# Filter-tap products regrouped by depth, four weight-split subtractions on GpSimd, and two small moves around them

## The chip, the cores and the metric

One core of a Trainium2 chip runs the whole layer as one program. The metric is the device time of one execution in microseconds (us); the median of three runs is given. One further execution was taken with the hardware profiler, and every row below is from that one.

## The reference, cut to what matters

The layer is a diffusion backbone block over 1024 tokens of width 1024, with 256 context tokens: normalisation, two parallel token mixers (a long convolution called Hyena and a recurrent mLSTM), a merge, then routing of tokens to 16 experts and a last normalisation. Four places matter here.

```python
# (1) the long filters: a small MLP gives h, its last layer is a product with w3
h = (h @ f32(w3)).reshape(L, HYENA_ORDER, 2, D_HYENA)
return h * jnp.exp(-t * deltas)[:, None, None, :]
# (2) routing: each of 16 experts takes its 128 best tokens
gate, idx = lax.top_k(jnp.swapaxes(aff, 1, 2), cap)
xg = h[bidx, idx]
# (3) the experts
a = jnp.einsum('becd,edf->becf', xg, w1); b = jnp.einsum('becd,edf->becf', xg, w3)
ye = jnp.einsum('becf,efd->becd', jax.nn.silu(a) * b, w2) * gate[..., None]
# (4) the last normalisation
return rmsnorm(x, final_norm_g)       # x * rsqrt(mean(x*x) + 1e-6) * g
```

## The kernel before, in words

Every large product runs on TensorE (PE) in three passes: an operand is split into a rounded high part and the remainder as low part, and high times high, high times low and low times high are summed in PSUM. A split is a cast on ScalarE (ACT) and a subtraction on VectorE (DVE) or GpSimd (POOL). PSUM has eight tiles of 128x512, which all stages share (`ps()`, line 125).

**Filters.** Eight units (kind, order, half of the channels) are made one after the other. `filter_taps` (line 384) makes a unit's taps: four PSUM tiles with two pairs of products each. Every pair is one product over 128 partitions (`hl` with `whh`) followed by one over 64 partitions (`hl` with `wll`, partitions 0 to 63 for the first four, 64 to 127 for the last four) into the same half of the tile. Each full tile is scaled out of PSUM by DVE (`fsf`), rounded by ACT and subtracted (`fs`; on DVE for the first unit, on POOL for the others). `filter_dft` (line 417) turns the taps into four PSUM tiles `fe`, and `filter_out` (line 437) combines these on DVE and POOL into `fk`, which goes to memory. `unit(u)` (line 555) runs the transform of unit u, the taps of unit u+2 and the output of unit u, with other small jobs interleaved (`ada`, the projection of the condition vector; the norms and transposes of the tokens). From the second unit on, the order of each engine's instructions is the planner's: it draws them by readiness and program order (`in_order[0] = False`, line 549); PE's order is the planner's from the start (`pe_order`).

**Routing.** The top 128 of each expert are found by DVE alone, sixteen rounds of MAX8, MATCH_REPLACE8 and FIND_INDEX8 (line 625 on). POOL then gathers the first expert's tokens by an indirect DMA (`gather`, line 1751), PE transposes them, and `gather_T` (line 1757) gives for each half n four scaled copies by ACT (`xgf`), a cast (`xgh`) and a subtraction (`xgl`).

**Experts.** 384 weight slabs of 1 MB flow through a ring of 11 tiles (`er`); `fill` (line 1724) splits each into `eh` (ACT) and `el` (DVE; only slab 2 on POOL). The first four slabs are split while the routing runs, ahead of `gather(0)` in program order. From line 1845 on, all engines keep program order until the last expert.

**Last norm.** For eight token tiles `xf` the sums of squares are made on ACT; `rsqrt` (line 477) for each pair of tiles is a chain of scale, square root on ACT, reciprocal, two multiplications, scale and multiplication on DVE; `last` (line 1923) scales the tiles, of which tiles 0, 2 and 4 are multiplied by the norm's weights on POOL, and stores them by the queue of SP.

Of the kernel before, what the change touches and what calls it, by code (L numbers as in the profile page):

```python
# [10 lines left out]
F32 = mybir.dt.float32  # L11
# [4 lines left out]
AF = mybir.ActivationFunctionType  # L16
OP = mybir.AluOpType
# [4 lines left out]
D = 1024  # L22
# [6 lines left out]
EPS = 1e-6  # L29
# [74 lines left out]
def layer_kernel(ctx: ExitStack, tc: tile.TileContext, A: dict, out: bass.AP, dbg=None, stop=None):  # L104
    nc = tc.nc
    in_order, pe_order = [True], [False]
    V, S, G = (InOrder(tc, e, in_order) for e in (nc.vector, nc.scalar, nc.gpsimd))
    T = InOrder(tc, nc.tensor, pe_order)
# [8 lines left out]
    def phase(st, name, side=None):  # L117

        pool = st.enter_context(tc.tile_pool(name=name, bufs=1, reuse_waits="tile", side=side))

        def alloc(shape, dt=F32, name=None, tag=None, bufs=1):
            return pool.tile(shape, dt, name=name, tag=tag or name, bufs=bufs)
        return alloc

    def ps(name="ps"):
        return pp.tile([128, 512], F32, name=name, tag="ps")

    def w2(shape, dt=F32, name="w"):
        return wk.tile(shape, dt, name=name, tag="w2", bufs=12)

    def sm(shape, name="sm"):
        return wk.tile(shape, F32, name=name, tag="sm", bufs=16)
# [14 lines left out]
    def bcast_row(ap, n):  # L147

        return bass.AP(tensor=ap.tensor, offset=ap.offset, ap=[[0, 128], [1, n]])

    def flat(name):
        a = A[name]
        n = 1
        for s in a.shape:
            n *= s
        return bass.AP(tensor=a.tensor, offset=a.offset, ap=[[1, n]])
# [227 lines left out]
    def filter_taps(u, al):  # L384

        kind, o, hf = u
        sets = [[al([128, 4, 256], F32R, name="fs", tag=f"ss{units.index(u) % 2}", bufs=4) for _ in range(2)] for _ in range(2)]
        filt["taps", u] = sets
        hl, whh, wll = filt["hl"], filt["whh"], filt["wll"]
        cs = slice(hf * 256, (hf + 1) * 256)  # L390
        for j2 in range(4):
            p = ps()
            h_ = slice(64 * (j2 // 2), 64 * (j2 // 2) + 64)
            for j in range(2):
                jt = j2 * 2 + j
                pj = p[:, j * 256:(j + 1) * 256]
                T.matmul(pj, hl[:, jt * 128:(jt + 1) * 128], whh[:, o, kind, cs], start=True, stop=False)
                T.matmul(pj, hl[h_, jt * 128:(jt + 1) * 128], wll[h_, o, kind, cs], start=False, stop=True)
            f = w2([128, 2, 256], name="fsf")
            js = slice((j2 % 2) * 2, (j2 % 2) * 2 + 2)  # L400
            V.scalar_tensor_tensor(f, p.rearrange("p (j c) -> p j c", j=2), -1.0 if kind and j2 > 1 else 1.0,
                                   filt["dec"][:, j2 * 2:j2 * 2 + 2, cs], op0=OP.mult, op1=OP.mult)
            if kind == 0 and j2 == 0:
                V.tensor_tensor(f[0:1, 0, :], f[0:1, 0, :], filt["skip"][:, o, cs], op=OP.add)
            hi, lo = sets[j2 // 2]
            S.copy(hi[:, js], f)
            (V if u == units[0] else G).tensor_tensor(lo[:, js], f, hi[:, js].bitcast(F32), op=OP.subtract)
            yield
# [68 lines left out]
    def rsqrt(ss, n, inv):  # L477

        v = sm([128, n], name="rq_v")
        V.tensor_scalar(v, ss, inv, EPS, op0=OP.mult, op1=OP.add)  # L480
        r = sm([128, n], name="rq_r")
        S.activation(r, v, AF.Sqrt)
        V.reciprocal(r, r)
        V.tensor_tensor(v, v, r, op=OP.mult)
        V.tensor_tensor(v, v, r, op=OP.mult)
        V.tensor_scalar(v, v, -0.5, 1.5, op0=OP.mult, op1=OP.add)
        V.tensor_tensor(r, r, v, op=OP.mult)
        return r
# [20 lines left out]
    late = phase(ctx, "late")  # L509
# [28 lines left out]
    def norm_tokens(*ii):  # L538
# [7 lines left out]
        yield  # L546

    run((filter_taps(units[0], alB), 1))
    in_order[0] = False
    filt["last_layer"](1)  # L550
# [491 lines left out]
    f = flat("b_in")  # L1042
# [90 lines left out]
    AB2 = late([128, 2, 8], F32, name="AB2")  # L1133
# [10 lines left out]
    p = ps()  # L1144
# [335 lines left out]
    for i in range(16):  # L1480
        p = ps()
# [17 lines left out]
    xs = []  # L1499
# [74 lines left out]
    for q in range(2):  # L1574
        for tt in range(8):
# [3 lines left out]
            i = q * 8 + tt  # L1579
# [38 lines left out]
    p = ps()  # L1618
# [27 lines left out]
    p = ps()  # L1646
# [17 lines left out]
    RAW, PAIR = 11, 4  # L1664
# [7 lines left out]
    def raw_tile(i):  # L1672
        return slot("er", i, RAW, [128, 2, 1024])

    def pair_tiles(i):
        return slot("eh", i, PAIR, [128, 2, 1024], F32R), slot("el", i, PAIR, [128, 2, 1024], F32R)
# [25 lines left out]
    def one(name, shape, dt=F32):  # L1702
        t = ring.pop((name,), None)
        return al(shape, dt, name=name) if t is None else t
# [16 lines left out]
    raws, pairs = [], []  # L1721
    taken = [0]

    def fill(n):

        while True:
            while len(raws) < min(len(pairs) + RAW, len(slabs)):
                raw = raw_tile(len(raws))
                SY.dma_start(raw, slabs[len(raws)].rearrange("(k p) n -> p k n", p=128))
                raws.append(raw)  # L1730
            i = len(pairs)
            if i >= min(n + PAIR, len(slabs)):
                return
            hi, lo = pair_tiles(i)
            S.copy(hi, raws[i])
            (G if i == 2 else V).tensor_tensor(lo, raws[i], hi.bitcast(F32), op=OP.subtract)
            pairs.append((hi, lo))


# [11 lines left out]
    def gather(e):  # L1751
        xg = one("xg", [128, 1024])
        G.indirect_dma_start(out=xg, out_offset=None, in_=xn_d,
                             in_offset=bass.IndirectOffsetOnAxis(ap=idxc[:, e:e + 1], axis=0))
        return xg

    def gather_T(xg):

        gh, gl = one("xgh", [128, 8, 128], F32R), one("xgl", [128, 8, 128], F32R)
        for n in range(2):  # L1760
            p = ps()
            for k in range(4):
                T.transpose(p[:, k * 128:(k + 1) * 128], xg[:, (n * 4 + k) * 128:(n * 4 + k + 1) * 128], ident)
            f = w2([128, 4, 128], name="xgf")
            ks = slice(n * 4, n * 4 + 4)

            def high(p=p, f=f, n=n, ks=ks):
                for k in range(4):
                    kk = n * 4 + k
                    S.activation(f[:, k], p[:, k * 128:(k + 1) * 128], AF.Identity, scale=AB2[:, 0, kk:kk + 1],  # L1770
                                 bias=AB2[:, 1, kk:kk + 1])
                S.copy(gh[:, ks], f)

            on_act.append(high)
            on_dve.append(lambda f=f, ks=ks: V.tensor_tensor(gl[:, ks], f, gh[:, ks].bitcast(F32), op=OP.subtract))
        return gh, gl
# [58 lines left out]

    fill(0)
    xg = gather(0)
    xs = {0: gather_T(xg)}
    for todo in (on_act, on_dve):
        while todo:  # L1840
            todo.pop(0)()
# [4 lines left out]
    for i in range(len(steps) + 1):  # L1846
        if i < len(steps):
            e, h = steps[i]
            if h == 0 and e + 1 < NE:
                xg = gather(e + 1)  # L1850
# [32 lines left out]
    def spare(shape, dt=F32, name=None):  # L1883

        n_raw[0] += 1
        return al(shape, dt, name=name, tag=f"er{(n_raw[0] - 1) % RAW}")

    warm = late([128, 1], F32, name="warm")
    tg = spare([128, 2, 1024], name="tg")
    SY.dma_start(tg[:, 0], bcast_row(A["tok"], 1024))  # L1890
    xf = []
    for i in range(4):
        t = spare([128, 2, 1024], name="xf")
        for j in range(2):
            tt = 2 * i + j
# [12 lines left out]
    sq = spare([128, 8, 2], name="sq")  # L1908

    later, rs2 = [], {}  # L1910
# [6 lines left out]
    def parts(tt):  # L1917

        if tt not in held:
            return [(xf[tt], slice(0, 1024))]  # L1920
        return [(held[tt][n], slice(n * 512, (n + 1) * 512)) for n in range(2)]
# [19 lines left out]
    for tt in range(8):  # L1941
        xt, on_pe = xf[tt], tt in (0, 7)
        if on_pe:
            held[tt] = [ps(), ps()]
            for n in range(2):
                T.matmul(held[tt][n], ident, xt[:, n * 512:(n + 1) * 512], start=True, stop=False)
        for n in range(2):
            p = held[tt][n] if on_pe else ps()
            for v in range(2):
                T.matmul(p, hot[:, tt * 128:(tt + 1) * 128], yhl[:, v, n], start=(v == 0 and not on_pe), stop=(v == 1))  # L1950
            if not on_pe:
                V.tensor_tensor(xt[:, n * 512:(n + 1) * 512], p, xt[:, n * 512:(n + 1) * 512], op=OP.add)
        for i, (src, ns) in enumerate(parts(tt)):
            S.activation(w2([128, 1024], BF16, name="junk")[:, ns], src, AF.Square, accum_out=sq[:, tt, i:i + 1])
        if on_pe:
            V.tensor_tensor(sq[:, tt, 0:1], sq[:, tt, 0:1], sq[:, tt, 1:2], op=OP.add)
        if tt % 2 == 1:
            rs2[tt - 1] = rsqrt(sq[:, tt - 1:tt + 1, 0], 2, 1.0 / D)
            if tt > 1:
                last(tt - 3)  # L1960
    last(6)
# [25 lines left out]
```

## Time and profile before

| what | value |
|---|---|
| median of three runs | 2297.56 us (2296.01 to 2298.42) |
| the profiled execution, its own time | 2295.03 us |
| its span, first to last instruction | 2293.3 us |
| PE busy | 2172.0 us, 95% |
| DVE busy | 1687.1 us, 74% |
| ACT busy | 1246.8 us, 54% |
| POOL busy | 443.5 us, 19% |

The profiled execution is 2.5 us below the median, and 1.7 us of it lie outside the span. A busy PE can be a PE that waits inside its pipeline, since ends of matmuls are modelled; so its share says little, and the steps between the starts of neighbouring products say more. In a row of a timeline stand the start in us, the duration, the engine, the operation with the tiles it writes and reads, the shape, the count, and in brackets the idle time of that engine before it with what ended it. In a table of stretches stand the stretch, its length, the busy time of PE, of PE's weight loads (PEld), DVE, ACT and POOL, each with its count, then PE's granted clock, the DMA share and GB/s; an engine with nothing in any stretch has no column.

### The profile page before, as it was taken

To read this page: it belongs to the slowest core of one execution; us is meant where nothing else is said; L and a number is where in the kernel's file an instruction comes from. 1 tells how busy PE (TensorE), PEld (TensorE's weight loads), DVE (VectorE), ACT (ScalarE), POOL (GpSimd) and SP (SyncE) were. 2 spreads that over 40 slices of the span, in tenths; PEclk is the share of its full clock that TensorE was granted. 3 is DMA by queue.
4 is the path that set the end of the run, shared out by engine and by line. 5 is a ranking of instruction groups with operands and counts; after the bars stand their busy time and mean duration, and the time that the engine had idled before them with its cause. 6 is when DMAs were issued, how large, how long until landed. Compare 5 with 4: busy or idle time off the path is not lost. (4 is left out here: it accounts for less than half of the span.)

```text
span 2293.3 us, 28327 instructions
## 1 busy us (share of the span) xinstructions
PE 2172.0 (95%) x10609; PEld 1772.4 (77%) x10609; DVE 1687.1 (74%) x1863; ACT 1246.8 (54%) x1398; POOL 443.5 (19%) x382
## 2 busy tenths in 40 slices
PE   6999999999999999999379999999999999999996
PEld 3679887787778788887268888888888888888884
DVE  5784445664446768553869889898888898888897
ACT  2441342324542223222257777777877777777774
POOL 3563101111124544042200111100111100011001
PEclk9879999999999999999689999999999999999998
DMA  7243335555563333864769999999999999999993
GB/s 264 93 139 95 113 114 176 176 195 190 177 199 114 110 115 124 300 223 147 271 216 386 380 386 382 378 379 393 381 385 384 379 377 396 380 386 383 380 349 141
DMA packets 234793, 605.18 MB, mean 264 GB/s; under 512 B 17722, under 2 KB 89462, under 8 KB 231456
## 3 DMA queue, kind: packets, MB, share of 16 engines
q1 hardware_dynamic: 216752, 551.44, 65.7%
q0 software_dynamic: 12128, 41.43, 5.7%
q10 hardware_dynamic: 5776, 10.50, 1.2%
q8 instruction: 83, 1.36, 0.2%
q14 instruction: 54, 0.44, 0.1%
HBM read 539.34 MB, written 63.98 MB: 263 GB/s over the span
## 5 line engine op out<-in xcount | busy, mean ns | idle before, releaser
L98 DVE TENSOR_TENSOR el<-er,eh 128x2048 fp32r<-128x2048 f32 x383 | 874.4, 2290 | 115.4 <-ACT eh L98 102.5
L98 ACT CAST eh<-er 128x2048 fp32r<-128x2048 f32 x384 | 733.7, 1915 | 236.6 <-PE pup L98 169.1
L98 PE MATMUL pup<-eh,xgh 128*128 128x512 f32 x1024 | 319.7, 393 | 1.6 <-ACT xgh L98 1.6
L98 PE MATMUL pup<-eh,xgl 128*128 128x512 f32 x1024 | 316.7, 390 | 0.0
L98 PE MATMUL ps<-hx,whi 128*128 128x512 f32 x960 | 305.4, 399 | 0.0
L98 PE MATMUL pup<-el,xgh 128*128 128x512 f32 x1024 | 274.4, 390 | 0.0
L98 PEld LDWEIGHTS pup<-eh,xgl 128*128 128x128 f32 x1024 | 192.7, 188 | 40.9 <-DVE xgl L98 0.2
L98 PEld LDWEIGHTS pup<-el,xgh 128*128 128x128 f32 x1024 | 192.6, 188 | 40.4
L98 PEld LDWEIGHTS pup<-eh,xgh 128*128 128x128 f32 x1024 | 190.3, 188 | 40.4 <-ACT xgh L98 2.0
L98 PEld LDWEIGHTS ps<-hx,whi 128*128 128x128 f32 x960 | 178.8, 189 | 40.3 <-ACT nt L98 0.8
L98 POOL DMA_INDIRECT acc_d<-ye,idxc x15 | 50.8, 3390 | 747.5 <-DVE ye L98 747.5
L98 PE MATMUL ps<-hx,wlo 128*128 128x512 f32 x480 | 189.9, 396 | 0.0
L98 PE MATMUL acc<-eh,gh 128*128 128x512 f32 x512 | 161.6, 397 | 0.2 <-ACT gh L98 0.2
L98 PE MATMUL acc<-eh,gl 128*128 128x512 f32 x512 | 160.2, 394 | 0.0
L98 PE MATMUL acc<-el,gh 128*128 128x512 f32 x512 | 139.5, 394 | 0.0
L98 PEld LDWEIGHTS acc<-eh,gl 128*128 128x128 f32 x512 | 96.0, 188 | 22.9 <-DVE gl L98 0.4
L98 PEld LDWEIGHTS acc<-el,gh 128*128 128x128 f32 x512 | 96.2, 188 | 22.4
L98 PEld LDWEIGHTS acc<-eh,gh 128*128 128x128 f32 x512 | 95.0, 188 | 21.6 <-ACT gh L98 0.5
L98 PEld LDWEIGHTS ps<-hx,wlo 128*128 128x128 f32 x480 | 90.5, 188 | 21.2
L98 PE MATMUL pg<-hx,gwh 128*128 128x512 f32 x320 | 103.2, 405 | 3.7 <-ACT gwh L98 3.7
L98 ACT ACTIVATE pb<-ps,colv 128x512 f32<-128x512 f32 (+1 forms) x44 | 29.3, 665 | 129.9 <-PE ps L98 122.2
L98 POOL DMA_INDIRECT xg<-xn_d,idxc x16 | 44.9, 2806 | 260.2 <-PE ps L98 226.1
(374 smaller groups left out, 3393.2 us busy)
## 6 DMA issues: line engine op xcount, KB each, us to landing
er<-in_w_exp_dram SPq DMA_DIRECT2D x384, 1024.0 KB, 7.6
wada<-in_w_ada_dram SPq DMA_DIRECT2D x24, 1024.0 KB, 5.0
wraw<-in_w_in_dram SPq DMA_DIRECT2D x30, 512.0 KB, 4.3
K_d<-fk SPq DMA_DIRECT2D x32, 256.0 KB, 2.2
Kt<-K_d SPq DMA_DIRECT2D x16, 512.0 KB, 5.7
v1c<-v_d SPq DMA_DIRECT2D x20, 256.0 KB, 8.0
gwr<-in_w_in_dram SPq DMA_DIRECT2D x20, 256.0 KB, 6.3
eo_d<-eost POOLq DMA_DIRECT2D x16, 256.0 KB, 7.0
```

What stands on the lines that cost most here:

```text
L98: r = op(*a, **k)
```

## The change

Four edits. In `filter_taps` all four PSUM tiles of a unit are taken at once, and its eight products over 128 partitions come first, then the eight over 64; only the first product of a tile sets the start flag. In `fill`, the subtractions of the first four slabs are all on POOL. In the first expert's `gather_T`, the four scaled copies of the second half are made by DVE instead of ACT. In the last norm a variant `rsqrt_s` takes the scale and the last affine step to ACT, each reading a constant tile `cs2`.

```diff
         hl, whh, wll = filt["hl"], filt["whh"], filt["wll"]
         cs = slice(hf * 256, (hf + 1) * 256)
+        pt = [ps() for _ in range(4)]
+
+        def tap(jt, high):
+            pj = pt[jt // 2][:, (jt % 2) * 256:(jt % 2 + 1) * 256]
+            h_ = slice(0, 128) if high else slice(64 * (jt // 4), 64 * (jt // 4) + 64)
+            T.matmul(pj, hl[h_, jt * 128:(jt + 1) * 128], (whh if high else wll)[h_, o, kind, cs], start=high and jt % 2 == 0, stop=not high and jt % 2 == 1)
+
+        for high in (True, False):
+            for jt in range(8):
+                tap(jt, high)
         for j2 in range(4):
-            p = ps()
-            h_ = slice(64 * (j2 // 2), 64 * (j2 // 2) + 64)
-            for j in range(2):
-                jt = j2 * 2 + j
-                pj = p[:, j * 256:(j + 1) * 256]
-                T.matmul(pj, hl[:, jt * 128:(jt + 1) * 128], whh[:, o, kind, cs], start=True, stop=False)
-                T.matmul(pj, hl[h_, jt * 128:(jt + 1) * 128], wll[h_, o, kind, cs], start=False, stop=True)
+            p = pt[j2]
...
             S.copy(hi, raws[i])
-            (G if i == 2 else V).tensor_tensor(lo, raws[i], hi.bitcast(F32), op=OP.subtract)
+            (G if i < PAIR else V).tensor_tensor(lo, raws[i], hi.bitcast(F32), op=OP.subtract)
...
-    def gather_T(xg):
+    def gather_T(xg, on=(True, True)):
...
-                    S.activation(f[:, k], p[:, k * 128:(k + 1) * 128], AF.Identity, scale=AB2[:, 0, kk:kk + 1],
-                                 bias=AB2[:, 1, kk:kk + 1])
+                    src, sc, sh = p[:, k * 128:(k + 1) * 128], AB2[:, 0, kk:kk + 1], AB2[:, 1, kk:kk + 1]
+                    if on[n]:
+                        S.activation(f[:, k], src, AF.Identity, scale=sc, bias=sh)
+                    else:
+                        V.tensor_scalar(f[:, k], src, sc, sh, op0=OP.mult, op1=OP.add)
...
-    xs = {0: gather_T(xg)}
+    xs = {0: gather_T(xg, (True, False))}
...
+    cs2 = late([128, 2], F32, name="cs2")
+    V.memset(cs2[:, 0:1], EPS)
+    V.memset(cs2[:, 1:2], 1.5)
+
+    def rsqrt_s(ss, n, inv):
+
+        v, r = sm([128, n], name="rq_v"), sm([128, n], name="rq_r")
+        S.activation(r, ss, AF.Sqrt, scale=inv, bias=cs2[:, 0:1])
+        S.activation(v, ss, AF.Identity, scale=inv, bias=cs2[:, 0:1])
+        V.reciprocal(r, r)
+        V.tensor_tensor(v, v, r, op=OP.mult)
+        V.tensor_tensor(v, v, r, op=OP.mult)
+        S.activation(v, v, AF.Identity, scale=-0.5, bias=cs2[:, 1:2])
+        V.tensor_tensor(r, r, v, op=OP.mult)
+        return r
...
-            rs2[tt - 1] = rsqrt(sq[:, tt - 1:tt + 1, 0], 2, 1.0 / D)
+            rs2[tt - 1] = rsqrt_s(sq[:, tt - 1:tt + 1, 0], 2, 1.0 / D)
```

## Rows read from the trace of the kernel before

**Rows 1.** A table of four stretches, all instructions (columns as told above).
```profile
54.00:90.00 36.00, 36.00 (x182) 23.26 (x180) 21.03 (x35) 13.90 (x25) 17.62 (x14) 0.91 0.43 150
90.00:121.00 31.00, 26.82 (x142) 21.42 (x142) 29.16 (x54) 14.13 (x29) 17.25 (x15) 0.76 0.21 69
121.00:146.00 25.00, 25.00 (x108) 19.77 (x108) 15.55 (x27) 12.77 (x23) 17.20 (x15) 0.70 0.25 85
146.00:184.00 38.00, 32.77 (x252) 31.54 (x251) 37.63 (x53) 20.52 (x29) 21.87 (x17) 0.94 0.61 182
```
**Rows 2.** PE's timeline: the first unit's tap products, first row and what follows.
```profile
24.70 0.58 PE L98 MATMUL ps<-whh,hl 128*128 128x256 f32 x1
...
32.86 1.86 PE L98 MATMUL ps<-fw,fh 64*1 64x512 f32 x2
```

**Rows 3.** PE's timeline: transform products, slow and quick, then the fifth unit's taps.
```profile
63.29 0.63 PE L98 MATMUL fe<-fs,fth 128*128 128x256 f32 x2
...
63.93 0.63 PE L98 MATMUL fe<-fs,fth 128*128 128x256 f32 x2
...
84.07 0.40 PE L98 MATMUL fe<-fs,fth 128*128 128x256 f32 x2
...
84.43 0.40 PE L98 MATMUL fe<-fs,fth 128*128 128x256 f32 x2
...
85.31 0.39 PE L98 MATMUL ps<-whh,hl 128*128 128x256 f32 x1
...
85.94 0.39 PE L98 MATMUL ps<-whh,hl 128*128 128x256 f32 x1
```

**Rows 4.** The tap products alone, busy in eight stretches, one per unit: sum.
```profile
sum 66.00, PE 50.37 PEld 28.76 DVE 0.21 ACT 0.00; mean PE 6.30 PEld 3.60 DVE 0.03 ACT 0.00
```

**Rows 5.** DVE's timeline in the first unit; PE's timeline at the first transform product.
```profile
34.76 0.68 DVE L98 TENSOR_TENSOR skip<-skip,ps 1x512 f32<-1x512 f32 x1 [5.49 <-PE ps L98]
...
41.70 0.68 DVE L98 TENSOR_TENSOR fs<-fsf,fs 128x512 fp32r<-128x512 f32 x1
...
44.68 0.79 PE L98 MATMUL fe<-fs,fth 128*128 128x256 f32 x2
```

**Rows 6.** The table of one stretch for the tile el alone: PE, PEld, DVE, POOL.
```profile
1113.00:1152.00 39.00, 0.00 (x0) 0.00 (x0) 6.79 (x3) 4.52 (x1) 0.50 0.72 272
```

**Rows 7.** DVE's timeline in the top-k rounds.
```profile
1119.70 0.67 DVE L98 MAX8 vals<-aw 48x8 f32<-48x512 f32 x1
...
1121.75 0.67 DVE L98 MAX8 vals<-aw 48x8 f32<-48x512 f32 x1
1122.34 2.26 DVE L98 TENSOR_TENSOR el<-er,eh 128x2048 fp32r<-128x2048 f32 x1
```

**Rows 8.** POOL's timeline from the first slab to the gather.
```profile
1116.65 4.52 POOL L98 TENSOR_TENSOR el<-er,eh 128x2048 fp32r<-128x2048 f32 x1 [0.89 <-ACT eh L98]
1155.33 1.03 POOL L98 DMA_INDIRECT xg<-xn_d,idxc  x1 [34.17 <-DVE idxl L98]
```

**Rows 9.** ACT's timeline: the first expert's scaled copies.
```profile
1161.04 1.86 ACT L98 ACTIVATE xgf<-ps,AB 128x128 f32<-128x128 f32 x5 [42.68 <-issue]
```

**Rows 10.** The last norm: a multiplication on POOL and a scale on DVE.
```profile
2278.02 2.34 POOL L98 TENSOR_TENSOR xf<-xf,tg 128x1024 f32<-128x1024 f32 x1 [1.54 <-ACT xf L98]
...
2278.12 2.26 DVE L98 TENSOR_SCALAR rq_v<-rq_v 128x2 f32<-128x2 f32 x1
```

**Rows 11.** An earlier norm: a subtraction on POOL and a small multiplication on DVE.
```profile
145.16 1.29 POOL L98 TENSOR_TENSOR fs<-fsf,fs 128x512 fp32r<-128x512 f32 x1 [0.40 <-ACT fs L98]
...
145.22 1.25 DVE L98 TENSOR_TENSOR rq_r<-rq_r,rq_v 128x2 f32<-128x2 f32 x1
```

**Rows 12.** After the first transform: PE's timeline, then DVE's.
```profile
54.45 0.28 PE L98 MATMUL ps<-whh,hl 128*128 128x256 f32 x1
...
62.84 1.28 DVE L98 TENSOR_TENSOR fk_t<-fe,fk_d 128x512 f32<-128x512 f32 x2
```

## The prediction

> **What bounds the kernel now.** I first asked where PE waits at all, since it is the busiest engine, and then, for each edit, which engine ends its own stretch last. From the end of the filters to the routing and through all experts PE runs without gaps worth naming, so what is won before such a stretch is kept through it. Three places are left, and the edits are in these three. In the filters the table of stretches [rows 1] shows a change of rule. From 54 to 90 us PE has no idle time and DVE works 21.0 of 36 us: PE is the limit. From 90 to 121 DVE works 29.2 of 31: DVE is the limit. From 121 to 146 it is PE again (25.0 of 25, DVE 15.6), and from 146 to 184 DVE again (37.6 of 38). In the routing, PE does nothing and DVE's chain of rounds is all that runs. In the last norm DVE's chain of small steps and POOL's three multiplications end it.
>
> **Regrouping the tap products.** The first unit's 16 products run from 24.70 to 32.86 [rows 2]: 8.16 us, 0.51 a product. In the fifth unit a pair takes 0.63 (85.31 to 85.94), so 0.31 a product [rows 3]. The transform's products have as many columns and are all of one depth. [...] The tap products cost 0.19 and 0.30 more than their columns explain, and what sets them apart is that each differs in depth from the one before. That is the price of a change of depth. It is paid 16 times a unit now and twice after the edit.
>
> With 14 products at the dense price and two at the present one a unit takes 14 x 0.12 + 2 x 0.31 = 2.3 us quick, or 14 x 0.21 + 2 x 0.51 = 4.0 slow. The first two units run slow. The eight bursts are busy 50.4 us [rows 4]; after, 2 x 4.0 + 6 x 2.3 = 21.8. So PE is freed of about 28 us. No row shows two 64-partition products behind each other. The bounds are the dense price and the present one; with the present one for all eight, a unit takes 8 x 0.12 + 8 x 0.31 = 3.4 (slow 5.8), the sum is 32, and 18 are freed. I take the dense price, because the transform's rows are the nearest case of products of one depth in a row.
>
> The row shows 0.31 where depth alternates against 0.12 where it doesn't. [...]
>
> How much of the 28 is on the path is read stretch by stretch.
> - Units 0 and 1: PE alone would start the first transform 2 x 4.16 = 8.3 us sooner. DVE's part waits 5.49 us for the product that stands behind unit 0's taps [rows 5]; it then runs to 42.4, and moves 4.2 sooner with unit 0 alone, to 38.2. The transform begins at 44.68 [rows 5] and would begin at 36.4; its later half needs the last of DVE's results. I take 7, near PE's end, as its first half doesn't need them.
> - Units 2 to 4, in the stretch where PE is the limit: 16 x 0.31 = 5.0 less 2.3 is 2.7 each. DVE has 15 us of room there, so 8 pass.
> - Unit 5, where DVE is the limit: 0.
> - Units 6 and 7: on average (50.4 - 16.5) / 6 - 2.3 = 3.3 each. DVE has 9 us of room, but its evictions now start after ten products instead of two, and from 146 it is the limit. I take half, 3.3.
>
> Together 18 us. The bounds are 2 (nothing passes but half of unit 0's lead) and 27. Taking four PSUM tiles at once costs nothing as long as a bank is free: four go to the transform, four to the taps, and a ninth tile (`ada`) makes one of the last four wait for the first eviction, 0.7 us. If that cover fails, it is the rival below.
>
> **Subtractions on POOL.** Three on DVE lie in the middle of the rounds, 6.79 us [rows 6], less the overlap with their neighbours (a MAX8 of 0.67 is followed after 0.59, [rows 7]), about 0.16 each: 6.3 us off DVE's chain, the only one that runs. On POOL one takes 4.52. Four in a row from 1116.65 end at about 1134.8; behind them on POOL's queue stands the gather at 1155.33 [rows 8], which would come at 1149, so 14 us cover it. SP's loads of the next slabs wait for these subtractions and are 14 us from being missed in the same way. Whether POOL slows the rounds: MAX8 takes 0.67 beside POOL's subtraction (1119.70) and 0.67 after it (1121.75) [rows 7]. So 6.3 are won; the bounds are 6.8 and 0 (POOL's queue late by the planner's order).
>
> **The second half's copies.** Five copies on ACT take 1.86 [rows 9], 0.37 each, and one of the second half stands ahead of the first half's cast: 0.4 off the path. DVE is idle there. If its four copies stand ahead of the first subtraction they may cost about 0.5 instead. I take -0.4.
>
> **The last norm.** DVE's scale of two elements takes 2.26 us, and ends with POOL's multiplication (2278.02 + 2.34) [rows 10]; it waits for POOL. There are three such waits, one for each multiplication, so at most 3 x 2.1 = 6.3 can go. But a small multiplication with both inputs in SBUF waits just so, 1.25 us beside POOL's 1.29 [rows 11], and these stay on DVE. What is late next is that multiplication. The two steps that go to ACT queue there behind the squares of whole tiles, whose price no row here gives; I bound it by one more wait as long as POOL's 2.34. I take -0.5, with bounds -4 and +2. [...] The two memsets of `cs2` are under 0.2 us and have no reader until then.
>
> **Sum.** 18 + 6.3 + 0.4 + 0.5 = 25 us off the profiled execution's 2295.0: 2270. That execution lies 2.5 under the median, so I predict 2272 for the median.
>
> **The rivals.**
> 1. Only part of the freed PE time arrives: 64-partition products keep the price of a change, or DVE takes over earlier than the stretches say. For it: DVE is full in two of the four. Against it: 15 and 9 us of room in the others. With 18 of 28 freed the path keeps about 11; 11 + 7 = 18 gives 2280. If PE, with less to do, is granted the slow level for two more transforms of 48 products, 2 x 48 x 0.09 = 9 us of PE come back, and with half of that on the path it is 2284.
> 2. The order on PE is not the one written. It is the planner's, and a 64-partition product is ready as soon as its partner is done. Then the first part is worth nothing, and 7 are left: 2290. Against it: PE follows the written order in all eight bursts before.
> 3. Slower: PE stalls on PSUM. A unit's seventh product needs the fourth bank. If that is one which `filter_out` must free, and DVE's steps come in the present order, PE waits from the transform's end (54.45) to 62.84 and more [rows 12], less six products: about 7 us a unit. For six units that is 42 against the 25 won: 2314. It decides from a wait of about 4 us a unit. Against it: two of the banks are freed by ACT copies that need nothing but the transform.
> 4. The planner's new order costs some us in a later stretch that the edits don't touch. No row can exclude it; it widens the range.
>
> **How the numbers follow.** Forecast 0.62, rival 1 0.22, rival 2 0.06, rival 3 0.05, rival 4 0.05 (from +5 to +30). The forecast's own range goes from 2260 (27 of PE time, 6.8 and 4) to about 2277. Rival 1 fills it up to 2288, rival 2 lies just above. I give 2260 to 2289, which leaves out about 0.15. A change of 0.2%, 4.6 us, is about what can be told from none. The subtractions alone exceed it, so faster has 0.88; same 0.06 and slower 0.06 come from rivals 3 and 4 and from late stretches that eat what is won.
>
> **What would show it.** Tap products of one depth at steps of 0.12 or 0.21, and eight bursts of 22 us in all. The first transform at about 37. The rounds without `el`, and the gather 6.3 us nearer to the first round. In the last norm the waits on `rq_v` multiplications in place of scales. Wrong it would be if PE's time in the filters falls and the first projection doesn't come 15 us or more sooner, or if POOL's four subtractions end after the gather's indices are ready.

## The result, and the profile after

The changed kernel takes 2262.03 us (median of 4 runs, 2258.0 to 2264.63), against 2297.99 us for the kernel before on the same chip (4 runs, 2296.01 to 2302.77): a ratio of 0.9843, 95% interval 0.9829 to 0.9858. Forecast were 2272.0 us and a range of 2260 to 2289. The direction is right and the time lies in the range, but near its lower end: 10 us more were won than the likeliest case said.

The profiled execution takes 2262.09 us, with a span of 2260.4. Against the profiled execution before that is 32.9 us, and all terms below add up to this. The head of its page, with the busy time of each engine:

```profile
span 2260.4 us, 28331 instructions
PE 2135.5 (94%) x10609; PEld 1754.4 (78%) x10609; DVE 1681.5 (74%) x1858; ACT 1246.4 (55%) x1402; POOL 457.1 (20%) x385
```

Following the lead from place to place shows where it came from. The times are starts, in us from the start of the span, read from the timelines of the two kernels:

| place | before | after | lead |
|---|---|---|---|
| first transform (unit 0) | 44.68 | 34.30 | 10.4 |
| second transform | 62.48 | 47.27 | 15.2 |
| third transform | 76.60 | 56.63 | 20.0 |
| fourth transform | 90.67 | 67.83 | 22.8 |
| fifth transform | 105.08 | 87.32 | 17.8 |
| sixth transform | 128.49 | 104.16 | 24.3 |
| seventh transform | 143.58 | 114.67 | 28.9 |
| first projection | 162.41 | 134.54 | 27.9 |
| first MAX8 of the routing | 1113.55 | 1087.64 | 25.9 |
| first expert's gather | 1155.33 | 1123.22 | 32.1 |
| first expert's product | 1163.46 | 1131.17 | 32.3 |
| last expert's output on DVE | 2261.71 | 2229.28 | 32.4 |
| end of the span | 2293.3 | 2260.4 | 32.9 |

So the filters give 28 us, of which 26 are left at the routing; the rounds give 6.2; the first expert's copies 0.2; the last norm 0.5. The taps of unit k + 2 run between the transforms of units k and k + 1, which lets each step of the table be put down to a unit. The first projection in PE's timeline, before and after:

```profile
162.41 0.39 PE L98 MATMUL pj<-whi,hch 128*128 128x264 f32 x1 [2.83 <-ACT whi L98]
```
```profile
134.54 0.59 PE L98 MATMUL pj<-whi,hch 128*128 128x264 f32 x1 [1.36 <-ACT whi L98]
```

The table of stretches answers to [rows 1]; its stretches lie at the same times but hold later work:

```profile
54.00:90.00 36.00, 27.69 (x185) 21.22 (x185) 32.41 (x60) 17.42 (x34) 18.50 (x15) 0.84 0.35 117
```

From 54 to 90 us PE had no idle time and DVE worked 21.0; now PE works 27.7 and DVE 32.4. DVE has become the limit there.

PE's timeline of units 0 and 1 answers to [rows 2], and with its last line to [rows 5]:

```profile
24.73 2.08 PE L98 MATMUL ps<-whh,hl 128*128 128x256 f32 x8
26.73 1.23 PE L98 MATMUL ps<-wll,hl 64*128 64x256 f32 x8
27.90 1.86 PE L98 MATMUL ps<-fw,fh 64*1 64x512 f32 x2
29.69 2.07 PE L98 MATMUL ps<-whh,hl 128*128 128x256 f32 x8
31.70 1.23 PE L98 MATMUL ps<-wll,hl 64*128 64x256 f32 x8
...
34.30 0.50 PE L98 MATMUL fe<-fs,fth 128*128 128x256 f32 x2
```

A unit took 8.16 us and takes 3.2. The eight products over 128 partitions stand 0.21 apart, as forecast for the slow level. The eight over 64 take 1.23 together, less than eight products of the dense price (8 x 0.21 = 1.7). All bursts together, as the one row over the stretch that holds them, answer to [rows 4] (50.37):

```profile
24.00:150.00 126.00, 24.47 (x128) 0.89 0.54 193
```

One caution on the clock column: the traces hold no record of the clock ahead of its first rise (48.2 us before, 33.8 after), and the tables then print 1.00. The steps of 0.21 in the first two units show the slow level there: in the kernel before, the transform's products stand at such steps where the clock is 0.50 (63.20 to 64.00).

The sixth unit (unit 5) is where lead is lost. PE's timeline and then DVE's, from its taps to its transform; the brackets give idle time and what ended it:

```profile
77.22 0.50 PE L98 MATMUL ps<-whh,hl 128*128 128x256 f32 x2 [1.76 <-DVE fk_t L98]
78.54 1.22 PE L98 MATMUL ps<-whh,hl 128*128 128x256 f32 x4 [0.82 <-DVE fk_t L98]
82.38 0.77 PE L98 MATMUL ps<-whh,hl 128*128 128x256 f32 x2 [2.61 <-DVE adac L98]
...
87.32 0.80 PE L98 MATMUL fe<-fs,fth 128*128 128x256 f32 x2 [3.02 <-DVE fsf L98]
```
```profile
83.93 1.42 DVE L98 TENSOR_SCALAR xt<-xt,rq_r 128x1024 f32<-128x1024 f32 x2
85.26 1.41 DVE L98 TENSOR_SCALAR xl<-xl,rq_r 128x1024 f32<-128x1024 f32 x2
86.58 2.48 DVE L98 SCALAR_TENSOR_TENSOR fsf<-ps,dec 128x512 f32<-128x512 f32 x4
```

Three times a tap product waits for a bank that DVE has yet to read, in all 5.2 us, and then the transform waits 3.0 for the evictions, which stand on DVE behind four scalings of token tiles.

In the routing, the table of the rounds for the tile `el` alone answers to [rows 6], POOL's timeline to [rows 8]:

```profile
1088.00:1126.00 38.00, 0.00 (x0) 0.00 (x0) 0.00 (x0) 17.93 (x4) 0.50 0.74 273
```
```profile
1089.95 17.93 POOL L98 TENSOR_TENSOR el<-er,eh 128x2048 fp32r<-128x2048 f32 x4
1123.22 1.03 POOL L98 DMA_INDIRECT xg<-xn_d,idxc  x1 [15.34 <-issue]
```

All four subtractions are on POOL and end at 1107.9, 15.3 us before the gather needs the queue. From the first MAX8 to the gather it is 35.58 us, against 41.79. (In the program before, the rounds stand at line 1627, not 625.)

In the last norm, POOL's multiplications and the small DVE step beside each answer to [rows 10]:

```profile
2239.49 2.61 POOL L98 TENSOR_TENSOR xf<-xf,tg 128x1024 f32<-128x1024 f32 x1 [30.34 <-ACT xf L98]
...
2245.63 2.34 POOL L98 TENSOR_TENSOR xf<-xf,tg 128x1024 f32<-128x1024 f32 x1 [3.53 <-ACT xf L98]
```
```profile
2239.81 2.31 DVE L98 TENSOR_TENSOR rq_v<-rq_v,rq_r 128x2 f32<-128x2 f32 x1
...
2245.79 2.40 DVE L98 TENSOR_TENSOR rq_v<-rq_v,rq_r 128x2 f32<-128x2 f32 x2
```

The scale no longer waits; the multiplication of two elements behind it does, as long as the scale did.

### The profile page after: what moved, and what is told of

Same layout as the page of the kernel before. It is cut to its first block, busy times and chain, and to the rows that moved or that the text cites. A ratio compares the mean times of both kernels' runs of the same rounds, so it can differ in the third digit from the quotient of the medians.

```text
span 2260.4 us, 28331 instructions
## 1 busy us (share of the span) xinstructions
PE 2135.5 (94%) x10609; PEld 1754.4 (78%) x10609; DVE 1681.5 (74%) x1858; ACT 1246.4 (55%) x1402; POOL 457.1 (20%) x385
## 4 chain that ended last, share of the span: by engine, by line
PE 49%; ACT 1%; DVE 0%; issue 0%; DVEq 0%; ACTq 0%
PE pup L98 31%; PE acc L98 16%; PE ps L98 2%; DVE rq_v L98 0%; ACT junk L98 0%; DVE xf L98 0%; DVEq L2005 0%; ACT rq_v L98 0%; ACT xf L98 0%; DVE rq_r L98 0%; ACT xgf L98 0%; ACT L98 0%; ACT xgh L98 0%; ACT gh L98 0%; ACT rq_r L98 0%
## 5 line engine op out<-in xcount | busy, mean ns | idle before, releaser
L98 PEld LDWEIGHTS acc<-eh,gl 128*128 128x128 f32 x512 | 96.1, 188 | 22.8 <-DVE gl L98 0.4
```

Of the source, the lines that this page charges most:

```text
L98: r = op(*a, **k)
```

## Experiments

Each median stands beside that of the kernel before on the same chip. The kernel before itself moved between 2293 and 2298 us from chip to chip, so ratios are compared, and for parts of a few us the intervals of the trace.

**One part at a time.** `taps_only` has the regrouped products and nothing else of the change, `sub_only` only this line:

```diff
-            (G if i == 2 else V).tensor_tensor(lo, raws[i], hi.bitcast(F32), op=OP.subtract)
+            (G if i < PAIR else V).tensor_tensor(lo, raws[i], hi.bitcast(F32), op=OP.subtract)
```

> The regrouped tap products alone; subtractions, first expert's copies and last norm as before. Theory A (the three parts add up and don't touch each other): all that the changed kernel won up to the routing, 26 us in its trace, is kept to the end, the rounds stay as long as before, so about 2270 us; the eight bursts are busy 24 us and the eight transforms 53 us instead of 61. Rival B (the later parts are hidden behind the earlier one or need it, so that the change's whole 36 us come from the taps): about 2262. Rival C (the taps' gain is given back in the routing when POOL's subtractions are missing): above 2275.

> The first four slabs' subtractions on GpSimd alone, all else as before. Theory A (parts add up): the routing's rounds are 6.2 us shorter, everything ahead of them is as before, about 2291.8 us; no el on DVE between the first MAX8 and the last round, and the gather starts without waiting for POOL. Rival B: the rounds shorten only together with the earlier start of the stage, under 2 us: 2296 to 2298.

Measured: `taps_only` 2268.51 us, ratio 0.9891 (0.987 to 0.9912); `sub_only` 2288.22 us, ratio 0.9977 (0.9961 to 0.9993). In the trace of `taps_only` the first projection starts at 134.8 as in the changed kernel, and the rounds take 41.79 us as before. In that of `sub_only` the filters are as before, and the rounds take 35.57. So 25 us and 5 us by the medians, 30 in sum against 36 for the whole (32 in `after_again` below), inside what the intervals leave open; in the traces the parts add up and neither needs the other: theory A for both. The copies and the norm's new steps have no run of their own, but the traces with and without them divide cleanly. From the first copy to the first product it is 2.41 us in the three traces with the old copies (`before` and these two) and 2.25 or 2.26 in the eleven others. From the last expert's output to the end it is 31.6 to 31.7 in the three with the old norm and 31.1 in the nine with the new one.

**What the old order paid for.** Two things set the old taps apart: each product differs in depth from the one before, and each second product adds to the PSUM region just written. `pairs_128` keeps the old order, and with it the second, but runs the second products over all 128 partitions (the edit against the kernel before):

```diff
         for j2 in range(4):
             p = ps()
...
-                T.matmul(pj, hl[h_, jt * 128:(jt + 1) * 128], wll[h_, o, kind, cs], start=False, stop=True)
+                T.matmul(pj, hl[:, jt * 128:(jt + 1) * 128], wll[:, o, kind, cs], start=False, stop=True)
```

> As the changed kernel, but each tap's second product follows the first one directly again, as before the change, and goes over all 128 partitions, so that no product differs in depth from the one before; the 64 partitions more add only the product of the two low parts, which the first kernel leaves out. Theory A (the price of the old order was the change of depth): 16 products at steps of 0.12 quick or 0.21 slow, 2 to 3.5 us a unit, first transform at about 34.5, time within 4 us of the changed kernel, 2258 to 2266. Rival B (the price was that the second product adds to the PSUM region that the first one has just written): steps of 0.31 or 0.51 stay, 6 to 8 us a unit, first transform at about 44, time about 2290.

Measured: 2260.1 us, ratio 0.9854 (0.9833 to 0.9876). PE's timeline in unit 0, its first four products:

```profile
24.67 0.58 PE L98 MATMUL ps<-whh,hl 128*128 128x256 f32 x1
25.05 0.41 PE L98 MATMUL ps<-wll,hl 128*128 128x256 f32 x1
25.27 0.41 PE L98 MATMUL ps<-whh,hl 128*128 128x256 f32 x1
25.48 0.41 PE L98 MATMUL ps<-wll,hl 128*128 128x256 f32 x1
```

The steps are 0.21 where the alternating order has 0.51 [rows 2], with the same regions in the same order. The old price was the change of depth, and rival B falls; what a change is spent on, no run shows. The whole gain of the regrouping comes without any regrouping. All bursts are busy 21.6 us, the first projection starts at 132.55, 2.0 before the changed kernel's.

**The eight cheap products.** `group_128` has the changed kernel's order exactly, with the second products over 128 partitions. `one_half` has that order too, with 64-partition products that all read the lower half, so that taps 4 to 7 leave out the product of their features' high part with `wll`:

```diff
-            h_ = slice(0, 128) if high else slice(64 * (jt // 4), 64 * (jt // 4) + 64)
+            h_ = slice(0, 128) if high else slice(0, 64)
```

> As the changed kernel, in exactly its order on PE, but the eight second products also go over all 128 partitions: no change of depth is left, and no two products can run side by side in the two halves of the partitions. Theory A (two changes of depth a unit at 0.15 to 0.2 each, and the eight low products running in pairs, nearly cancel): a unit's burst 3.4 us instead of 3.13 at the slow clock, 2.0 instead of 2.3 at the quick one; time within 2 us of the changed kernel. Rival B (the eight in 1.23 us are only how the trace shows them and the pairs don't exist): the burst is shorter by two changes of depth at both clocks, 2.8 us in the first unit. Rival C (the pairs matter more than the changes): bursts 0.5 us or more longer each, 3 us or more slower.

> As the changed kernel, in its order on PE, but all eight second products of a unit read partitions 0 to 63, so that taps 4 to 7 are computed with the low part of their features in place of the high part; the work has the same size. Theory A (the products of the two halves of the partitions run side by side, which made eight cost 1.23 us at the slow clock and let the first two units take 3.2 us each instead of the 4.0 forecast): with one half only they run one after the other at 0.2 us, the eight take 1.8 to 2.0 us, a unit about 3.9, and the first transform starts 1.3 us later than in the changed kernel. Rival B (64-partition products are cheap by themselves): 1.2 us for eight as before, the first transform where it was.

Measured: `group_128` 2259.16 us, ratio 0.9848 (0.983 to 0.9866); `one_half` 2264.76 us, a single run. The eight second products of unit 0 in PE's timelines, of `group_128` and then of `one_half`:

```profile
26.59 1.91 PE L98 MATMUL ps<-wll,hl 128*128 128x256 f32 x8
```
```profile
26.70 2.07 PE L98 MATMUL ps<-wll,hl 64*128 64x256 f32 x8
```

With one half they take 2.07 instead of 1.23, and the first transform starts 2.1 us later, at 36.37: theory A of `one_half`. In the changed kernel the trace has these products in pairs 0.01 us apart and the pairs at 0.2 to 0.38, although in the program the four of the lower half all stand ahead of the four of the upper: products on the two halves of the partitions run side by side. They are reported finished in program order all the same: of the second pair, which ends at 27.53 and 27.54, only one tile's semaphore counts up at once, at 27.54; the next counts come at 27.97, 28.01 and 28.05, so the upper half's first tile is told of behind the lower half's second, 0.47 us after its end. `group_128` shows that the pairs and the two remaining changes of depth nearly cancel over the eight units, 23.9 us against 24.5, but not at each level: a unit's burst is 3.8 us instead of 3.2 at the slow clock (I had 3.4), which is rival C's half microsecond, and 2.34 instead of 2.47 at the quick one. By the time, 0.9848 against 0.9843 and 0.9864 for the changed kernel, it is theory A.

**PE's time against its clock.** The eight transforms are the same work in all kernels, but busy 60.7 us before and 53.0 after (54.6 in `after_again`). `filler` adds dense products to the changed kernel, `two_units` takes the regrouping out of units 2 to 7:

```diff
+        for _ in range(16 if u in units[:2] else 22):
+            T.matmul(pt[0][:, 0:256], hl[:, 0:128], whh[:, o, kind, cs], start=True, stop=True)
         for high in (True, False):
```
```diff
+        pt = []
+        if u in units[:2]:
+            pt = [ps() for _ in range(4)]
...
         for j2 in range(4):
-            p = pt[j2]
+            if pt:
+                p = pt[j2]
+            else:
+                p = ps()
+                h_ = slice(64 * (j2 // 2), 64 * (j2 // 2) + 64)
+                for j in range(2):
...
```

> As the changed kernel, but ahead of a unit's eight products over 128 partitions stand 16 more of them (units 0 and 1) or 22 more (the others), whose result is overwritten: about as many us of PE work as the old order's changes of depth cost, without a change of depth. Theory A (the freed PE time is what pays; the transforms' 8 us less came from the new order of the taps): bursts of 6.5 and 5 us, some 45 us in all; the transforms stay at 53 us; first transform 6.8 us later than in the changed kernel, first projection about 20 us later, time about 20 us over the changed kernel, 0.993 of the kernel before. Rival B (the transforms' 8 us come with a shorter stretch as a whole, and return when the taps are long again): transforms at 60 us, first projection 27 us later, 0.995 to 0.997. Rival C (DVE limits the units after the first two, PE's time there is spare): first projection only 7 us later, 0.988.

> As the changed kernel, but only the first two units' products are regrouped; units 2 to 7 have the old order. Theory A (each stretch keeps what it wins): first transform 10.4 us sooner than before, the lead stays about 10 to the first projection, transforms about 60 us; with the routing's 6.2 and 0.7 of the rest 17 us under the kernel before, 0.9925. Rival B (the lead is eaten where DVE is the limit, in units 5 to 7, as DVE's work is not less): lead of 3 us at the first projection, 10 us under before, 0.9955. Rival C (most of the gain comes from here, as the early start moves the slow clock's stretches too): lead over 18 us, 0.989.

Measured: `filler` 2273.45 us, ratio 0.9906 (0.9888 to 0.9924); `two_units` 2278.93 us, ratio 0.9929 (0.9909 to 0.9949). The transforms alone, one row over all eight, with PE's busy time and, behind the count, the granted clock of the stretch: before, after, `two_units`, `filler`.

```profile
30.00:175.00 145.00, 60.67 (x384) 0.86 0.44 149
```
```profile
30.00:175.00 145.00, 53.02 (x384) 0.91 0.48 166
```
```profile
30.00:175.00 145.00, 59.50 (x384) 0.84 0.46 158
```
```profile
30.00:175.00 145.00, 52.91 (x384) 0.94 0.46 160
```

`two_units` and `filler` have nearly as much tap work, 42.0 and 39.1 us, yet the transforms are 6.6 us apart. So their time doesn't follow from how long the taps are, but from their order. Tables of short stretches around two bursts of alternating products in `two_units`, and two dense ones in `filler`, show where the clock (the number behind the count) falls:

```profile
57.70:61.80 4.10, 4.10 (x15) 0.99 1.03 342
61.80:68.60 6.80, 6.80 (x24) 0.50 0.04 17
74.70:78.80 4.10, 4.10 (x15) 1.00 0.19 62
78.80:85.70 6.90, 6.90 (x24) 0.51 0.00 1
```
```profile
58.40:64.50 6.10, 6.10 (x43) 1.00 0.71 262
72.60:78.60 6.00, 6.00 (x46) 1.00 0.40 133
```

In `two_units` it falls from 1.00 to 0.50 inside the bursts, with no pause of PE shown, and stays there through part of the transform that follows. Four of the kernel before's five slow stretches ahead of the first projection begin in such a burst, at 58.4, 102.8, 126.7 and 140.4; the bursts of units 3 and 4 have none. In `filler` none of three does; in the changed kernel one begins as PE waits in unit 5's taps, at 78.2. All fourteen traces divide in the same way. In the three whose units 2 to 7 alternate (`before`, `sub_only`, `two_units`) the transforms take 59.5 to 60.7 us, and 13 slow stretches begin without a pause of PE shown shortly ahead of them, inside 11 of the 18 bursts or within 0.7 us behind two more. In the eleven others they take 52.5 to 55.6, and each slow stretch ahead of the first projection begins behind a pause of PE. So the alternating order cost twice, in the products themselves and in the clock of the transforms behind them. Why the clock falls in these bursts, and not in every one, no run shows.

`filler` also tells how much of PE's time is on the path: 14.6 us of tap work more delay the first projection by 12.0, or 0.8 of it. That lies between theory A's 20 (which had also taken the filler at a slower clock) and rival C's 7, and so does the ratio. The first transform comes 1.6 us later, not 6.8: unit 1's 32 products take 3.8 us, so they ran at the quick level already. `two_units` keeps 8.9 of its first transform's 10.1 us to the first projection: theory A.

**The sixth unit.** `late_scale` puts the scalings of four token tiles behind the fourth unit's output steps in the program, `pairs_late` does the same to `pairs_128`:

```diff
-    unit(3, (ag0, 1), (nt, 1))
+    unit(3, (ag0, 1), (some(nt, 4), 1))
+    for _ in nt:
+        pass
```

> As the changed kernel, but the scaling of the fourth to seventh token tile stands, in the program, behind the fourth unit's output steps instead of between them: on DVE one of four scalings, not four, is then ahead of the sixth unit's evictions (0.7 us each). Theory A (in the sixth unit DVE's queue is what ends last, and gives 5 us back): PE's wait of 3.0 us ahead of the fifth transform shrinks by about 2, and the stage up to the first projection ends 1 to 2 us sooner. Rival B (it only moves the wait to the next unit's DVE steps): the fifth transform 2 us sooner, the sixth and the first projection as in the changed kernel. In total time neither can be told from the changed kernel, 0.984 to 0.985.

> The version with each pair of products over 128 partitions one behind the other, together with the late scaling of the token tiles: evictions can start after the first four products of a unit, and in the sixth unit they stand ahead of all four scalings on DVE. Theory A (both shorten the stretch in which DVE is the limit): first projection at 130 to 132 us after the start, against 134.5 in the changed kernel and 132.7 with the pairs alone; time 2 to 4 us under the changed kernel, 0.9825 to 0.984. Rival B (the scalings are then late for the seventh unit's transposes, whose wait takes their place): first projection at 132.7 or later, 0.985.

Measured: `late_scale` 2262.21 us, ratio 0.9865 (0.9844 to 0.9886); `pairs_late` 2262.44 us, ratio 0.9862 (0.9842 to 0.9881). PE's timeline of `late_scale`, the fifth transform's waits:

```profile
85.67 0.79 PE L98 MATMUL fe<-fs,fth 128*128 128x256 f32 x2 [1.03 <-DVE fsf L98]
...
92.89 0.51 PE L98 MATMUL fe<-fs,fth 128*128 128x256 f32 x2 [1.66 <-DVE fk_t L98]
...
98.27 0.50 PE L98 MATMUL fe<-fs,fth 128*128 128x256 f32 x2 [3.24 <-DVE hxf L98]
```

The wait for the evictions shrinks from 3.02 to 1.03 us, and the fifth transform starts 1.7 us sooner. But waits for DVE's next steps come in its place, and the sixth transform and the first projection are 0.5 later than in the changed kernel, of which 0.35 stand at the first transform already: rival B. `pairs_late` does no better than `pairs_128` (first projection at 133.4 against 132.6). As far as these two orders show, DVE's whole work is the limit in this stretch, and not its order.

**The last norm without POOL.** `no_pool` scales and multiplies tiles 0, 2 and 4 on DVE in one step, as the others are (tile 0 in two halves); `pairs_no_pool` joins it to `pairs_128`; `after_again` is the changed kernel on the same chip:

```diff
-                if tt in (0, 2, 4):
-                    S.activation(xt[:, ns], src, AF.Identity, scale=r)
-                else:
-                    V.scalar_tensor_tensor(xt[:, ns], src, r, tg[:, 1, ns], op0=OP.mult, op1=OP.mult)
-            if tt in (0, 2, 4):
-                G.tensor_tensor(xt, xt, tg[:, 1], op=OP.mult)
...
+                V.scalar_tensor_tensor(xt[:, ns], src, r, tg[:, 1, ns], op0=OP.mult, op1=OP.mult)
+            store(tt)
```

> The changed kernel itself, once more, on the chip of the two runs beside it, so that they can be compared directly: 0.9843 of the kernel before, 0.983 to 0.987; rounds 35.6 us from the first MAX8 to the gather, last norm 31.1 us from the first scaled expert output to the end of the span, as in its first trace; the start of the routing may lie some 4 us off by where the slow clock's stretches fall.

> As the changed kernel, but in the last norm the tiles 0, 2 and 4 are scaled by DVE in one instruction as the others are, in place of a scaling on ACT and a multiplication on GpSimd. Theory A (small DVE steps wait until GpSimd's multiplication is done, in the changed kernel as before it, only in other steps): without GpSimd no small step takes over 0.3 us; the three waits of 2.1 to 2.3 us go, three instructions of 1.28 come, the stretch from the first scaled expert output to the end is 31.1 - 3 x 2.15 + 3 x 1.28 = 28.5 us, total 2.6 us less than the changed kernel beside it. Rival B (the small steps are slow for a reason of their own, such as their operands): the three slow steps stay and the stretch is 31.1 + 3.8 = 35 us.

> The version with each pair of tap products over 128 partitions one behind the other, together with the last norm without GpSimd. Theory A (both add up): first projection 1.9 us sooner than in the changed kernel, last norm 2.6 us shorter: 4 to 5 us under the changed kernel beside it, 0.982 of the kernel before. Rival B (what is won in the filters is lost in where the slow clock's stretches fall): not to be told from the last norm's gain alone, 0.983 to 0.984.

Measured: `after_again` 2264.41 us (2261.77 to 2267.28), ratio 0.9864 (0.9839 to 0.9888); `no_pool` 2257.66 us (2255.65 to 2259.7), ratio 0.9827 (0.9807 to 0.9848); `pairs_no_pool` 2256.46 us (2255.01 to 2257.59), ratio 0.9827 (0.9806 to 0.9847). DVE's timeline of `no_pool`, the same small multiplication as above and the instruction ahead of it:

```profile
2239.20 0.73 DVE L98 SCALAR_TENSOR_TENSOR xf<-ps,rq_r,tg 128x512 f32<-128x512 f32 x1
2239.85 0.15 DVE L98 TENSOR_TENSOR rq_v<-rq_v,rq_r 128x2 f32<-128x2 f32 x1
```

It takes 0.15 us instead of 2.31. From the last expert's output to the end it is 28.1 us against 31.1 in both executions of the changed kernel, 3.0 less although DVE multiplies three more tiles: theory A, which had 28.5. In `pairs_no_pool` the first projection also starts 1.9 us sooner and the last norm is as short, which adds up in the trace; by the medians it can't be told from `no_pool` alone. No run of either `no_pool` version is as slow as the fastest of `after_again`; their medians lie 7 and 8 us under its median. Of these the norm explains 3.0; in the profiled executions `no_pool` is only 2.0 us shorter, as its routing starts 1.0 later. For the rest of the 7 no trace shows a cause.

## Why the prediction was right, and where a term was off

**The direction and three of the four terms.** The subtractions were to give 6.3 us and give 6.2, and `sub_only` shows the same rounds alone; POOL's queue has 15.3 us of cover where 14 were forecast. The copies were to give 0.4 and give 0.2 (first copy to first product 2.41 us before, 2.25 after). The last norm was to give 0.5, an estimate between bounds of -4 and +2, and gives 0.5; that the wait goes on to the multiplication and is not won is in the rows, and `no_pool` shows POOL as its cause. The multiplication takes 2.31 us beside POOL's and 0.15 without it. The scale of the kernel before took 2.14, 2.26 and 2.31 us beside POOL's three multiplications, each time ending within 0.03 us of POOL's end, and 0.17 where none ran (2285.18).

**The price of a change of depth** was read right: 0.19 to 0.30 us, `pairs_128` has the products at 0.21 without it. The dense price it is taken against, 0.12 and 0.21 us, is a third of the steps of 0.36 and 0.64 in [rows 3], two products with `fth` and one with `ftl`; the trace grants 1.00 of the clock at the first (84.05 to 84.50) and 0.50 at the second (63.20 to 64.00), which are the quick and the slow level. The bursts were to fall from 50.4 to 21.8 us and fall to 24.5, with the first two units below the forecast and the others above it (2.5 to 3.8 us each, where 2.3 was taken; units 5 and 6 ran partly at the slow level). Rival 2, another order on PE, did not come.

**The term that was off is how much of this is on the path: 18 us forecast, 27.9 at the first projection, 25.9 at the routing.** Step by step of that list:
- Units 0 and 1: 7 forecast, 10.4 measured. I had taken 4.0 us a unit and it is 3.2, because the eight 64-partition products run in pairs: 1.23 us, against 2.07 for eight of one half. `one_half`, without the pairs, takes 4.1 a unit and starts the transform 2.1 us later. The rest of the miss, 1.3, is DVE, on account of which I took 7 of 8.3: PE's full gain came through.
- Units 2 to 4: 8 forecast, 12.4 measured. The taps give 8.2 as forecast (15.65 to 7.4 us busy). The transforms between these places are 2.4 us quicker, and PE's other work there (9.1 to 7.3 us busy) gives the last 1.8. Waits of PE give nothing: the kernel before has none there.
- Unit 5: 0 forecast, and 5.0 are given back. DVE is the limit as the prediction said, but from earlier on: its rows show 5.2 us of waits for banks and 3.0 for evictions. This is the mechanism of rival 3, in one unit of six and at 5.2 us for its banks where it was priced at 7; the point from which it was to decide, 4 us in every unit, was never near, since units 2 to 4 have no such wait.
- Units 6 and 7: 3.3 forecast, 11.1 measured, the largest miss. The taps give 12.3 - 6.9 = 5.3 us there, and the two transforms between these places 4.0 more (19.4 to 15.4 us); of the last 1.8, half are waits of PE that went (4.2 to 3.3 us) and half is its other work. I had let half of the taps' part through.

**The term that was missing is the clock.** I asked only whether PE, with less to do, would be slower (rival 1), and priced that at 9 us against the change. The transforms became 7.65 us quicker instead (6.1 in `after_again`). `two_units` and `filler` show that the alternating products had brought the slow level (0.50 and 0.51 in and behind two bursts of `two_units`), and that dense ones in nearly the same amount, 39.1 us against 42.0, did not: none of `filler`'s three slow stretches begins in a burst. A table of short stretches could have told it, here of the kernel before, PE alone, in and behind unit 2's burst (54.4 to 60.0):

```profile
54.40:58.40 4.00, 4.00 (x15) 1.00 0.64 259
58.40:65.20 6.80, 6.80 (x26) 0.50 0.34 104
```

The clock falls in the middle of the burst, while PE is busy all the time.

**Luck.** The forecast for the profiled execution was 2270.0 us, and it took 2262.09. The first projection's lead of 27.9 lies beyond the 27 that the prediction called its bound. The total stayed in the range partly by luck: units 0 to 4, 6 and 7 gave 16 us more than was credited to them, in part by the clock, which no term held; 5.0 lost in unit 5 and 3.0 behind the seventh transform, which no term held either, took half of that back.

**Rival 1** named two causes and a slow clock. The 64-partition products did not keep the price of a change (1.23 us for eight). DVE did take over earlier, in unit 5. The clock went the other way. Its size, 11 of 28 us, did not come: the lead is 27.9, and `filler` has 0.8 of added PE time on the path. **Rival 4** is not shown: between the first projection and the routing the lead of the changed kernel shrinks by 2.0 us, that of `taps_only` grows by 1.7, and that of `group_128` shrinks by 5.3. The time at the slow level in that part, 24.7, 21.0 and 30.6 us against 24.3 before, stands in the same order, as does PE's busy time (924.6, 920.7, 926.8; 923.7 before). Over all fourteen traces busy time grows with slow time too, if less strictly. So where the slow stretches fall goes with these differences; a cost of the planner's order need not be added, and can't be excluded.

## What to carry to other kernels

When products of two depths alternate on PE, price the change and not the columns (steps of 0.51 us here against 0.21 at the slow level), and look at the granted clock of the stretch behind, which fell to 0.50 here in the same order; padding the shallow product to the full depth did as well as regrouping (bursts of 21.6 us in `pairs_128`, 24.5 in the changed kernel). When a freed engine is credited with part of its time, write down which rows of the other engine limit it, unit by unit; "half" gave 3.3 us here where 11.1 came, 5.3 of it from the taps alone. A wait for another engine's instruction can move on to the next small step instead of going, as it did here from the scale (2.26 us) to the multiplication (2.31); it was won only when POOL's multiplications went (0.15).

## What the runs showed of the hardware

- Products over the two halves of the partitions ran side by side, also where in the program four of one half stood ahead of the other's four: eight in 1.23 us in the changed kernel's first unit, against 2.07 with one half alone (`one_half`). Their semaphores still counted up in program order (27.54, then 27.97, 28.01 and 28.05).
- In steady alternation a change of depth cost 0.30 us at a granted clock of 0.50 (steps of 0.51 against 0.21) and 0.19 at 1.00 (0.31 against 0.12); two in a unit of the changed kernel, with its pairs, left its burst within 0.15 us of `group_128`'s at 1.00 (2.47 against 2.34).
- In bursts of alternating products, shown without a pause, the granted clock fell to 0.50 (`two_units`, 61.8 to 68.6 and 78.8 to 85.7), in 11 of 18 such bursts of three traces; dense bursts kept it at 1.00 in five of the six of `filler`'s units 2 to 7 (58.4 to 64.5 and 72.6 to 78.6 among them), with a mean of 0.85 in the one at 109.0 to 114.2.
- A DVE multiplication of 128x2 took 2.31 us beside a POOL multiplication of 2.61 (changed kernel, 2239.81), and 0.15 without it (`no_pool`, 2239.85).
